# Opening of a decoder trunk: token tiles rounded one k tile at a time, two weight units loaded in pieces, outputs on two queues

## The chip, the cores and the metric

The kernel runs on one core of a Trainium2 chip. A core has a matrix engine (TensorE, PE in the profile), a vector engine (VectorE, DVE), an activation engine (ScalarE, ACT), a general engine (GpSimd, POOL) and a synchronisation engine (SyncE, SP) that here issues most memory transfers. Each engine takes its instructions in order; they wait for one another through semaphores. The metric is the time of one execution on the device in microseconds (us).

## The reference

A two-layer decoder over 256 tokens of width 1024. Every layer has two half-step SwiGLU networks around a token mixer, and each sub-layer is normalised on both sides:

```python
def rms_norm(x, g):
    xf = x.astype(jnp.float32)
    y = xf * lax.rsqrt(jnp.mean(xf * xf, axis=-1, keepdims=True) + EPS)
    return (y * g.astype(jnp.float32)).astype(x.dtype)

def swiglu(x, w_gate, w_up, w_down):
    return (jax.nn.silu(x @ w_gate) * (x @ w_up)) @ w_down

for layer in range(DEPTH):
    if layer == N_A_LAYERS:
        k, v, c = shared_kv(h, kv_norm_g, w_kv, w_fgate, b_fgate)
    f = swiglu(rms_norm(h, ffn1_pre_g[layer]), ffn1_w_gate[layer], ffn1_w_up[layer], ffn1_w_down[layer])
    h = h + 0.5 * rms_norm(f, ffn1_post_g[layer])
    hn = rms_norm(h, mix_pre_g[layer])
    m = recurrent_block(hn, ...) if layer < N_A_LAYERS else forgetting_attention(hn, ..., k, v, c)
    h = h + rms_norm(m, mix_post_g[layer])
    f = swiglu(rms_norm(h, ffn2_pre_g[layer]), ffn2_w_gate[layer], ffn2_w_up[layer], ffn2_w_down[layer])
    h = h + 0.5 * rms_norm(f, ffn2_post_g[layer])
```

The model width is 1024, the network width 2816. Everything is float32. The part that matters here is the very first product, the first network's `x @ w_gate` on normalised tokens, and the very last step, the sum into `h` that is the output.

## The kernel before

**Precision by two parts.** A float32 product is formed from three products of rounded operands. Each operand is split into an upper part (the value rounded to TensorE's format, `F32R`) and a lower part (the value minus its upper part, also rounded). The sum of upper by upper, upper by lower and lower by upper goes into one PSUM bank. ScalarE writes the upper part (a copy with rounding), VectorE the lower part (a subtraction).

**Tokens.** The 256 tokens are two halves (t = 0 and 1) of 128 rows, `h[0]` and `h[1]`. For a projection a half is turned on TensorE, 128 columns (one k tile) at a time, into a PSUM bank `gt` that holds four k tiles; there are two such banks. Then VectorE multiplies the four k tiles by the norm's weight `gT` into a scratch tile `xg` (L221), ScalarE rounds `xg` into `xhi` (L222), and VectorE writes `xlo` (L227). The root mean square itself is applied behind the product, as a factor per row (`stat`: a sum of squares on ScalarE, L204, then two small operations on GpSimd).

**Weights.** Weights come as units (items): a unit is two k tiles of 512 columns, 512 KB. It lands in one of five `raw` tiles, is split into `whi` and `wlo` (nine buffers each) by L174 and L175, and is used by both token halves, six products for each half. Each product is a 128x512 matrix product. Four units make one 128x512 result; the first four units are the first 512 columns of the first gate matrix, the next four those of the up matrix. Behind the opening the loop `run` walks the units with token half 0 ahead of half 1; in the first network half 0 takes units 4 to 7 before half 1 takes unit 4. A planner (`prepare_next`, with a modelled time `pace`, and `landed` and `split_at` for each unit) decides where in the program the split of a unit stands. TensorE's order is always the order of the program; in the opening that holds for all engines (`manual_schedule`).

**The opening** (L1091 to L1164) is an order written out by hand for the first four units and all sixteen token k tiles. SyncE loads the left half of `h[0]`, unit 0 in two pieces, the left half of `h[1]`, unit 1, the right half of `h[0]`, unit 2, the right half of `h[1]`, unit 3. The gain row (8 KB) is loaded by ScalarE's queue (L112). TensorE begins with four products on a zero tile (`keep_busy`, L126), turns the gain row, turns four k tiles of half 0, does three more zero products, and then goes through unit 0 and unit 1 by the strings in `FIRST`, each of which names a product by k tile in the unit, weight part and token part ("0ul" is k tile 0, upper weight, lower token). `turn_between` puts the transposes of the other four-tile groups between those products. Units 2 and 3 go through the ordinary `mm3`. The sums of squares stand behind the split of unit 3, and the split of unit 4 (L174) behind them. Then the two gate results go through SiLU (L474).

**The end.** `enter` with `last` forms the output rows in four pieces of 256 columns for each half (L259) and SyncE stores each piece (L261).

Of the kernel before, what the change touches and what calls it, by code (L numbers as in the profile page):

```python
# [9 lines left out]
F32 = mybir.dt.float32  # L10
# [6 lines left out]
P = 128  # L17
# [27 lines left out]
def trunk_kernel(ctx: ExitStack, tc: tile.TileContext, A: dict, out: bass.AP):  # L45
# [66 lines left out]
    nc.scalar.dma_start(grow0, A["ffn1_pre_g"].rearrange("l (k p) -> (l k) p", p=P))  # L112
# [6 lines left out]
    warm = cpool.tile([P, 1], F32, name="warm")  # L119
    nc.scalar.activation(warm, mhalf, AF.Silu)  # L120

    def keep_busy(n):
# [120 lines left out]
    def enter(t, dests, pf, gb, half, last=False, normed=False):  # L243
# [13 lines left out]
        for c in range(0, D, m):  # L257
            hn = h[t][:, c:c + m]
            nc.vector.scalar_tensor_tensor(hn, t1[c // 512][:, c % 512:c % 512 + m], r[:, 0:1], hn, ALU.mult, ALU.add)  # L259
            if last:  # L260
                nc.sync.dma_start(out[0, t * P:(t + 1) * P, c:c + m], hn)  # L261
        urgent.__exit__(None, None, None)
# [38 lines left out]
    def gain_bcast(src):  # L301
# [10 lines left out]
    OPEN = 4  # L312

    FIRST = {(0, 0): "0uu 0lu 0ul 1uu 1ul 1lu", (0, 1): "0uu 1uu 0ul 1ul 0lu 1lu",
             (1, 0): "0uu 1uu 0lu 1lu 0ul 1ul", (1, 1): "0uu 1uu 0lu 1lu 0ul 1ul"}
    between = {}
    first_loads = []
    landed = {}

# [41 lines left out]
    def proj_items(w, c0, nn, get_x, post, nk=8):  # L361
# [4 lines left out]
        for k0 in range(0, nk, kper):  # L366
# [7 lines left out]

            def work(t, u, k0=k0, kn=kn, i=len(items)):
                if k0 == 0:
                    acc[t] = mmbank()
                ps = acc[t][:, :nn]
                if (t, i) in FIRST:
                    for n, (j, a, b) in enumerate(FIRST[t, i].split()):  # L380
                        if (t, i, n) in between:
                            between.pop((t, i, n))()
                        j = int(j)
                        nc.tensor.matmul(ps, get_x(t, k0 + j)[b == "l"], (u.lo if a == "l" else u.hi)[:, j * nn:(j + 1) * nn],
                                         start=i == n == 0, stop=False)
                    return
# [5 lines left out]
            if not items:  # L392
                first_loads.append(lambda fetch=fetch: fetch(pieces=2))
            elif len(items) < OPEN:
                first_loads.append(fetch)
# [706 lines left out]
    def first_split(i, pieces=1):  # L1102

        u = units[i] = Unit()
        u.hi, u.lo = [wpool.tile([P, 1024], F32R, tag=s, name=nm(s), bufs=WB) for s in ("whi", "wlo")]
        m = 1024 // pieces

        def upper(c=0):
            nc.scalar.activation(u.hi[:, c * m:c * m + m], raws[i][:, c * m:c * m + m], AF.Copy)

        def lower(c=0):
            nc.vector.tensor_tensor(u.lo[:, c * m:c * m + m], raws[i][:, c * m:c * m + m],
                                    u.hi[:, c * m:c * m + m].bitcast(F32), ALU.subtract)
        return upper, lower

    dest = [main_dest(0, t) for t in range(2)]
    state["p"] = 2
    keep_busy(4)
    gains_T(grow0, 16, 0)
    tp00 = to_tp(h[0], 0)  # L1120
    keep_busy(3)
    upper, lower = first_split(0, 2)
    upper(0)
    x00 = x_upper(tp00, dest[0], 0)
    lower(0)
    x_lower(x00, dest[0], 0)
    upper(1)
    lower(1)
    tps = {}

    def turn_between(key, t, n):
        between[key] = lambda: tps.setdefault((t, n), to_tp(h[t], n))

    turn_between((0, 0, 3), 1, 0)
    half(0, 0)
    upper, lower = first_split(1)
    upper()
    lower()
    x10 = x_upper(tps[1, 0], dest[1], 0)
    turn_between((0, 1, 4), 0, 1)  # L1140
    half(0, 1)
    x_lower(x10, dest[1], 0)
    upper, lower = first_split(2)
    upper()
    x01 = x_upper(tps[0, 1], dest[0], 1)
    lower()
    turn_between((1, 0, 4), 1, 1)
    half(1, 0)
    x_lower(x01, dest[0], 1)
    x11 = x_upper(tps[1, 1], dest[1], 1)  # L1150
    half(1, 1)
    x_lower(x11, dest[1], 1)
    upper, lower = first_split(3)
    upper()
    lower()
    stat(0)
    stat(1)
    state["p"] = OPEN
    for i in range(OPEN):
        landed[i] = split_at[i] = pace["t"] - 2.0  # L1160
    for i in range(2, OPEN):
        half(0, i)
        half(1, i)
# [89 lines left out]
```

## Time and profile before

| | |
|---|---|
| runs | 1005.61, 1007.07 and 3560.49 us; median 1007.07 |
| profiled execution | 1005.73 us, of which the profile's span is 1004.0 |
| TensorE busy | 992.4 us of the span (99%) |
| VectorE, ScalarE busy | 618.1 us (62%), 529.9 us (53%) |
| data moved | 178.88 MB, mean 178 GB/s |
| first product of the opening | at 6.50 us |
| last product | begins at 997.04 us |

Times in the profile count from the start of the span. A timeline row gives the start, the duration, the engine, the line of the kernel, the operation with its output and inputs, the shape, and in brackets how long the engine had been idle and what released it. "PEld" is the weight load of TensorE; a matrix product's recorded duration overlaps with the next one, so the distance between two starts is what one product costs in a row. "SPq" and "ACTq" rows are transfers being issued, not moved. A group row gives the count, then the busy time and the mean duration in nanoseconds.

### The profile page before, as it was taken

The numbers are of one execution on the slowest core, as the hardware profiler recorded it, in microseconds if no ns is written. First come the engines' busy times: TensorE is split into PE (matmuls) and PEld (weight loads), VectorE is DVE, ScalarE is ACT, GpSimd is POOL, SyncE is SP. The second block draws the span as 40 slices with busy tenths as digits, with TensorE's granted clock in tenths as the row PEclk, the third lists the DMA queues.
The fourth block names the chain that finished last, engine by engine and source line by source line (L and its number), as shares of the span: only waits on it lengthen the run. The fifth ranks groups of instructions, "written<-read, shape, count | busy, mean of one in ns | idle before, by whom it ended". The sixth has DMA issues, their size and how long they took to land.

```text
span 1004.0 us, 12890 instructions
## 1 busy us (share of the span) xinstructions
PE 992.4 (99%) x4790; PEld 829.1 (83%) x4790; DVE 618.1 (62%) x761; ACT 529.9 (53%) x726; POOL 48.5 (5%) x94
## 2 busy tenths in 40 slices
PE   8999999999999999999999999999999999999997
PEld 5888888889988888888898888888888888888885
DVE  5756554668998555554686655554488475555542
ACT  6546443559986544443564444444466565444431
POOL 2400000000004000000100000000020000000000
PEclk9999999999999999999999999999999999999999
DMA  7877656565337766655567666555555067665531
GB/s 250 302 206 206 195 181 193 170 179 150 123 99 231 209 189 179 196 178 190 133 198 233 185 184 186 179 185 190 166 180 158 2 207 211 184 192 187 181 116 42
DMA packets 92628, 178.88 MB, mean 178 GB/s; under 512 B 11950, under 2 KB 32598, under 8 KB 92566
## 3 DMA queue, kind: packets, MB, share of 16 engines
q1 hardware_dynamic: 91702, 177.94, 57.4%
q8 instruction: 37, 0.61, 0.2%
q0 software_dynamic: 832, 0.12, 0.1%
q14 instruction: 25, 0.20, 0.1%
q10 hardware_dynamic: 32, 0.01, 0.0%
HBM read 176.95 MB, written 1.05 MB: 177 GB/s over the span
## 4 chain that ended last, share of the span: by engine, by line
PE 76%; issue 19%; ACT 2%; DVE 1%; POOL 1%; DMA 1%; SPq 0%; POOLq 0%; DVEq 0%; ACTq 0%
PE mm L182 22%; PE mm L184 22%; PE mm L183 22%; PE gt L717 2%; PE tr L489 1%; PE gt L1008 1%; PE mm L189 1%; PE mm L191 1%; PE mm L190 1%; PE mm L1035 1%; ACT junk L204 1%; DMA raw<-in_ffn_w_gate_dram 1%; PE gt L213 1%; PE tr L1024 0%; POOL rstd L199 0%
## 5 line engine op out<-in xcount | busy, mean ns | idle before, releaser
L175 DVE TENSOR_TENSOR wlo<-raw,whi 128x1024 fp32r<-128x1024 f32 (+4 forms) x329 | 395.7, 1207 | 269.5 <-ACT whi L174 267.8
L174 ACT ACTIVATE whi<-raw 128x1024 fp32r<-128x1024 f32 (+4 forms) x325 | 338.5, 1045 | 318.2 <-PE mm L184 254.0
L182 PE MATMUL mm<-whi,xhi 128*128 128x512 f32 (+2 forms) x776 | 307.6, 396 | 0.0
L184 PE MATMUL mm<-whi,xlo 128*128 128x512 f32 (+2 forms) x776 | 302.3, 390 | 0.0
L183 PE MATMUL mm<-wlo,xhi 128*128 128x512 f32 (+2 forms) x776 | 301.8, 389 | 0.2 <-DVE wlo L175 0.2
L184 PEld LDWEIGHTS mm<-whi,xlo 128*128 128x128 f32 x776 | 145.7, 188 | 30.7 <-DVE xlo L227 0.5
L183 PEld LDWEIGHTS mm<-wlo,xhi 128*128 128x128 f32 x776 | 146.1, 188 | 29.5 <-DVE wlo L175 1.2
L182 PEld LDWEIGHTS mm<-whi,xhi 128*128 128x128 f32 x776 | 145.9, 188 | 27.8
L182 PE MATMUL mm<-whi,hhi 128*128 128x512 f32 x352 | 139.2, 396 | 0.0
L184 PE MATMUL mm<-whi,hlo 128*128 128x512 f32 x352 | 137.9, 392 | 0.0
L183 PE MATMUL mm<-wlo,hhi 128*128 128x512 f32 x352 | 137.1, 389 | 0.0
L184 PEld LDWEIGHTS mm<-whi,hlo 128*128 128x128 f32 x352 | 66.1, 188 | 14.9
L183 PEld LDWEIGHTS mm<-wlo,hhi 128*128 128x128 f32 x352 | 66.2, 188 | 13.9
L182 PEld LDWEIGHTS mm<-whi,hhi 128*128 128x128 f32 x352 | 66.2, 188 | 13.1
L483 DVE SCALAR_TENSOR_TENSOR prod<-mm,rstd,sil 128x512 f32<-128x512 f32 (+1 forms) x48 | 33.9, 706 | 39.5 <-PE mm L184 35.8
L197 POOL TENSOR_SCALAR nv<-ss 128x1 f32<-128x1 f32 x24 | 11.6, 482 | 911.3 <-ACT junk L204 911.3
L474 ACT ACTIVATE sil<-mm,rstd 128x512 f32<-128x512 f32 (+1 forms) x48 | 31.3, 651 | 40.3 <-PE mm L184 40.3
L493 ACT ACTIVATE hhi<-tr 128x512 fp32r<-128x512 f32 (+1 forms) x48 | 26.6, 554 | 15.2 <-PE tr L489 15.1
L254 DVE TENSOR_TENSOR t<-mm,gb 128x512 f32<-128x512 f32 x24 | 16.2, 687 | 28.7 <-ACT junk L204 28.7
L204 ACT ACTIVATE junk<-mm 128x512 bf16<-128x512 f32 x24 | 14.2, 590 | 32.9 <-PE mm L184 32.8
L494 DVE TENSOR_TENSOR hlo<-tr,hhi 128x512 fp32r<-128x512 f32 (+1 forms) x48 | 30.5, 642 | 1.3
L182 PE MATMUL mm<-whi,zhi 128*128 128x340 f32 (+2 forms) x80 | 28.4, 355 | 0.0
(181 smaller groups left out, 907.1 us busy)
## 6 DMA issues: line engine op xcount, KB each, us to landing
raw<-in_ffn_w_down_dram SPq DMA_DIRECT2D x88, 512.0 KB
raw<-in_ffn_w_up_dram SPq DMA_DIRECT2D x80, 512.0 KB
raw<-in_ffn_w_gate_dram SPq DMA_DIRECT2D x79, 512.0 KB
raw<-in_rg_w_in_dram SPq DMA_DIRECT2D x20, 504.0 KB
raw<-in_rg_w_out_dram SPq DMA_DIRECT2D x10, 504.0 KB
raw<-in_ffn_w_gate_dram SPq DMA_DIRECT2D x18, 256.0 KB
raw<-in_ffn_w_up_dram SPq DMA_DIRECT2D x16, 256.0 KB
raw<-in_w_kv_dram SPq DMA_DIRECT2D x8, 512.0 KB
```

The source lines that it names most:

```text
L174: nc.scalar.activation(hi[:parts, c:c + m], rawv[:, c:c + m], AF.Copy)
L175: nc.vector.tensor_tensor(lo[:parts, c:c + m], rawv[:, c:c + m], hi[:parts, c:c + m].bitcast(F32), ALU.subtract)
L182: nc.tensor.matmul(ps, xh, wh, start=first, stop=False)
L183: nc.tensor.matmul(ps, xh, wl, start=False, stop=False)
L184: nc.tensor.matmul(ps, xl, wh, start=False, stop=last)
L204: nc.scalar.activation(junk[:, :src.shape[1]], src, AF.Square, scale=f, accum_out=acc)
L254: nc.vector.tensor_tensor(t1[n], pf[n], gb[:, n * 512:(n + 1) * 512], ALU.mult)
L474: nc.scalar.activation(s[:, :nn], ps, AF.Silu, scale=rs[t][:, 0:1])
L483: nc.vector.scalar_tensor_tensor(pr[:, :nn], ps, rs[t][:, 0:1], s, ALU.mult, ALU.mult)
L493: nc.scalar.activation(hv, tp[:, :nn], AF.Copy)
L494: nc.vector.tensor_tensor(lv, tp[:, :nn], hv.bitcast(F32), ALU.subtract)
L717: nc.tensor.matmul(ps[:w, j * S:(j + 1) * S], wv[:, o:o + w], xc[:w, k, :], start=k == 0, stop=k == m - 1)
```

## The change

The rest of the kernel keeps its order; on every engine only the opening and the last stores differ.

- `load_h` now takes k tile bounds and a queue. Half 0's left half is loaded in two pieces of two k tiles with the pieces of unit 0 between them; units 0 and 1 are loaded in pieces of one k tile. The left half of `h[1]` is loaded by ScalarE's queue, behind the warm-up activation.
- Tokens: the scratch tile `xg` is gone. ScalarE rounds each k tile on its own, straight from PSUM, with the norm's weight as the activation's scale (`x_up`); VectorE forms the lower part in one fused operation per k tile, again from PSUM (`x_lo`): sixteen operations on each engine.
- Weights of units 0 and 1 are split in pieces of one k tile; the upper part of the first piece of each is written by VectorE (`w_up(..., dve=True)`), not ScalarE.
- Products of all four units go by a written order (`products`). The first group of transposes is cut in two (`turn(0, 0, 2)` and `turn(0, 2, 4)`), the second standing behind the first two products. One zero product instead of three stands behind the first transposes, and only the half of the zero tile that is read is cleared.
- The splits of units 4 and 5 stand ahead of the sums of squares, that of unit 6 behind them, all three ahead of the two SiLUs.
- At the end, for half 1, the second and fourth of the four stores are issued by ScalarE's queue.

```diff
-    def load_h(t, n):
-        nc.sync.dma_start(h[t][:, n * 512:(n + 1) * 512], A["x"][0, t * P:(t + 1) * P, n * 512:(n + 1) * 512])
+    def load_h(t, a, b, q=nc.sync):
+        q.dma_start(h[t][:, a * P:b * P], A["x"][0, t * P:(t + 1) * P, a * P:b * P])
...
-    nc.vector.memset(idle, 0.0)
+    nc.vector.memset(idle[:, :512], 0.0)
...
     nc.scalar.activation(warm, mhalf, AF.Silu)
+    load_h(1, 0, 4, nc.scalar)
...
             if last:
-                nc.sync.dma_start(out[0, t * P:(t + 1) * P, c:c + m], hn)
+                q = nc.scalar if t == 1 and c % 512 else nc.sync
+                q.dma_start(out[0, t * P:(t + 1) * P, c:c + m], hn)
...
-    load_h(0, 0)
-    raws = [first_loads[0]()]
-    load_h(1, 0)
-    raws.append(first_loads[1]())
-    load_h(0, 1)
-    raws.append(first_loads[2]())
-    load_h(1, 1)
-    raws.append(first_loads[3]())
...
+    load_h(0, 0, 2)
+    load_w(0, 0, 1)
+    load_h(0, 2, 4)
+    load_w(0, 1, 2)
+    load_w(1, 0, 1)
+    load_w(1, 1, 2)
+    load_h(0, 4, 8)
+    load_w(2, 0, 2)
+    load_h(1, 4, 8)
+    load_w(3, 0, 2)
...
+    def w_up(i, a, b, dve=False):
+        c = slice(a * 512, b * 512)
+        if dve:
+            nc.vector.tensor_copy(parts[i][0][:, c], raws[i][:, c])
+        else:
+            nc.scalar.activation(parts[i][0][:, c], raws[i][:, c], AF.Copy)
...
+    def x_up(t, a, b):
+        for k in range(a, b):
+            nc.scalar.activation(xhi[:, k, t * P:(t + 1) * P], tps[t, k // 4][:, k % 4 * P:(k % 4 + 1) * P], AF.Copy,
+                                 scale=gT[:, k:k + 1])
+
+    def x_lo(t, a, b):
+        for k in range(a, b):
+            nc.vector.scalar_tensor_tensor(xlo[:, k, t * P:(t + 1) * P], tps[t, k // 4][:, k % 4 * P:(k % 4 + 1) * P],
+                                           gT[:, k:k + 1], xhi[:, k, t * P:(t + 1) * P].bitcast(F32),
+                                           ALU.mult, ALU.subtract)
+
+    def products(t, i, order):
+        for c in order.split():
+            j = int(c[0])
+            k = 2 * i + j
+            tensor_work(512)
+            nc.tensor.matmul(first_acc[t], main_x(t, k)[c[2] == "l"], parts[i][c[1] == "l"][:, j * 512:(j + 1) * 512],
+                             start=k == 0 and c[1:] == "uu", stop=k == 7 and c == order.split()[-1])
+
     keep_busy(4)
     gains_T(grow0, 16, 0)
-    tp00 = to_tp(h[0], 0)
-    keep_busy(3)
...
+    turn(0, 0, 2)
+    keep_busy(1)
+    x_up(0, 0, 2)
+    w_up(0, 0, 1, dve=True)
+    x_lo(0, 0, 1)
+    w_lo(0, 0, 1)
+    w_up(0, 1, 2)
+    x_lo(0, 1, 2)
+    w_lo(0, 1, 2)
+    products(0, 0, "0uu 0ul")
+    turn(0, 2, 4)
+    products(0, 0, "0lu 1uu 1ul 1lu")
+    turn(1, 0, 4)
+    x_up(1, 0, 2)
+    w_up(1, 0, 1, dve=True)
+    x_lo(1, 0, 2)
+    x_up(0, 2, 4)
+    w_lo(1, 0, 1)
+    products(1, 0, "0uu 0lu 1uu 1lu 0ul 1ul")
+    w_up(1, 1, 2)
+    x_lo(0, 2, 4)
+    x_up(1, 2, 4)
+    w_lo(1, 1, 2)
+    products(0, 1, "0uu 0lu 1uu 0ul 1ul")
+    turn(0, 4, 8)
+    products(0, 1, "1lu")
+    x_lo(1, 2, 4)
+    products(1, 1, "0uu 0lu 1uu 1lu 0ul 1ul")
+    w_up(2, 0, 2)
+    x_up(0, 4, 8)
+    w_lo(2, 0, 2)
+    turn(1, 4, 8)
+    x_lo(0, 4, 8)
+    products(0, 2, "0uu 1uu 0lu 1lu 0ul 1ul")
+    x_up(1, 4, 6)
+    w_up(3, 0, 2)
+    x_up(1, 6, 8)
+    x_lo(1, 4, 6)
+    w_lo(3, 0, 2)
+    x_lo(1, 6, 8)
+    products(1, 2, "0uu 1uu 0lu 1lu 0ul 1ul")
+    products(0, 3, "0uu 1uu 0ul 1ul 0lu 1lu")
+    products(1, 3, "0uu 1uu 0lu 1lu 0ul 1ul")
+    state["p"] = OPEN
+    for i in range(OPEN):
+        landed[i] = split_at[i] = pace["t"] - 3.0
+    for i in range(2):
+        prepare_next(True)
     stat(0)
     stat(1)
+    prepare_next(True)
...
```

`load_w(i, a, b)` loads k tiles a to b of unit i, `w_lo` writes the lower part of such a piece, `turn(t, a, b)` turns k tiles a to b of half t.

More of the change, by code (lines that the diff above doesn't have):

```diff
@@ L391, in work @@
                     post(t, acc[t][:, :nn])
-            if not items:
-                first_loads.append(lambda fetch=fetch: fetch(pieces=2))
-            elif len(items) < OPEN:
+            if len(items) < OPEN:
                 first_loads.append(fetch)
@@ new lines, in trunk_kernel, with w_lo @@
+    load_w(2, 0, 2)
+    load_h(1, 4, 8)
+    load_w(3, 0, 2)
+    parts = [[wpool.tile([P, 1024], F32R, tag=s, name=nm(s), bufs=WB) for s in ("whi", "wlo")] for _ in range(OPEN)]
+    def w_up(i, a, b, dve=False):
[4 more added lines that the diff above has]
+            nc.scalar.activation(parts[i][0][:, c], raws[i][:, c], AF.Copy)
+    def w_lo(i, a, b):
+        c = slice(a * 512, b * 512)
+        nc.vector.tensor_tensor(parts[i][1][:, c], raws[i][:, c], parts[i][0][:, c].bitcast(F32), ALU.subtract)
@@ new lines, in trunk_kernel, with turn @@
+    tps = {}
+    def turn(t, a, b):
+        n = a // 4
+        if (t, n) not in tps:
+            tps[t, n] = gtbank()
+        for k in range(a, b):
+            nc.tensor.transpose(tps[t, n][:, k % 4 * P:(k % 4 + 1) * P], h[t][:, k * P:(k + 1) * P], ident)
+    def x_up(t, a, b):
[3 more added lines that the diff above has]
+    def x_lo(t, a, b):
+        for k in range(a, b):
+            nc.vector.scalar_tensor_tensor(xlo[:, k, t * P:(t + 1) * P], tps[t, k // 4][:, k % 4 * P:(k % 4 + 1) * P],
+                                           gT[:, k:k + 1], xhi[:, k, t * P:(t + 1) * P].bitcast(F32),
+                                           ALU.mult, ALU.subtract)
@@ L1122, in trunk_kernel @@
[L1122 to L1142, printed above, removed]
@@ L1156, in trunk_kernel @@
     stat(0)
     stat(1)
-    state["p"] = OPEN
+    prepare_next(True)
     for i in range(OPEN):
-        landed[i] = split_at[i] = pace["t"] - 2.0
-    for i in range(2, OPEN):
+        units[i] = Unit()
         half(0, i)
```

46 lines of the change are left out of this document (10 added, 36 removed).

## The prediction

> **What bounds the kernel now.** I read the stretches first, then the timeline of the opening, then the groups that price single operations. The stretches (start and end, length, then busy time of each engine with its count, granted clock, DMA share, GB/s) show where TensorE idles:
>
> ```profile
> 0.00:20.00 20.00, 16.52 (x65) 10.37 (x66) 10.62 (x15) 10.41 (x16) 1.52 (x10) 1.00 0.75 263
> 20.00:28.00 8.00, 7.84 (x33) 5.73 (x32) 5.95 (x5) 6.85 (x8) 7.46 (x15) 1.00 0.76 211
> 28.00:100.00 72.00, 72.00 (x332) 59.27 (x331) 46.37 (x63) 39.48 (x45) 7.74 (x13) 1.00 0.77 239
> 100.00:990.00 890.00, 888.65 (x4333) 748.00 (x4332) 549.12 (x668) 471.05 (x653) 30.09 (x53) 1.00 0.56 173
> 990.00:1004.00 14.00, 7.44 (x33) 5.78 (x31) 6.07 (x12) 2.06 (x6) 1.72 (x4) 0.84 0.23 75
> ```
>
> From 28 to 990 us TensorE is busy 960.65 of 962. What can move lies in the first 28 us and in the last ten. So I follow one quantity: when TensorE reaches a fixed product behind the opening. I take the one at 27.86, the first after unit 7's first half; if it comes earlier, so does the end, since nothing behind it waits. The timeline (start, duration, engine, line, operation, in brackets the idle time before it and its releaser):
>
> ```profile
> 0.79 0.42 ACTq L112 DMA_DIRECT2D grow<-in_ffn_pre_g_dram  x1
> 2.53 0.20 ACT L120 ACTIVATE warm<-mhalf 128x1 f32<-128x1 f32 x1
> 3.65 0.26 PE L132 MATMUL tr<-ident,grow 16*128 16x16 f32 x1 [0.24 <-DMA grow<-in_ffn_pre_g_dram]
> 3.94 0.17 DVE L133 TENSOR_SCALAR gT<-tr 128x16 f32<-128x16 f32 x1 [2.48 <-PE tr L132]
> 3.94 1.12 PE L213 MATMUL gt<-ident,h 128*128 128x128 f32 x4
> 4.60 0.63 ACT L1109 ACTIVATE whi<-raw 128x512 fp32r<-128x512 f32 x1 [1.86 <-DMA raw<-in_ffn_w_gate_dram]
> 4.85 1.49 PE L126 MATMUL tr<-idle 128*128 128x512 bf16 x3
> 6.50 0.50 PE L384 MATMUL mm<-whi,xhi 128*128 128x512 f32 x1 [0.17 <-ACT xhi L222]
> 7.56 0.65 PE L213 MATMUL gt<-ident,h 128*128 128x128 f32 x4
> 8.28 0.39 PE L384 MATMUL mm<-whi,xlo 128*128 128x512 f32 x1
> 8.51 0.40 PE L384 MATMUL mm<-wlo,xhi 128*128 128x512 f32 x1
> 9.93 0.73 PE L384 MATMUL mm<-whi,xhi 128*128 128x512 f32 x2 [1.03 <-ACT whi L1109]
> 10.96 0.60 PE L213 MATMUL gt<-ident,h 128*128 128x128 f32 x4
> 11.32 0.71 PE L384 MATMUL mm<-wlo,xhi 128*128 128x512 f32 x2
> 12.46 0.73 PE L384 MATMUL mm<-whi,xhi 128*128 128x512 f32 x2 [0.42 <-ACT xhi L222]
> 16.64 1.04 ACT L1109 ACTIVATE whi<-raw 128x1024 fp32r<-128x1024 f32 x1
> 17.59 1.04 ACT L204 ACTIVATE junk<-h 128x1024 bf16<-128x1024 f32 x1
> 18.75 1.06 ACT L204 ACTIVATE junk<-h 128x1024 bf16<-128x1024 f32 x1
> 19.81 1.04 ACT L174 ACTIVATE whi<-raw 128x1024 fp32r<-128x1024 f32 x1
> 20.76 0.67 ACT L474 ACTIVATE sil<-mm,rstd 128x512 f32<-128x512 f32 x1
> 21.33 1.05 ACT L174 ACTIVATE whi<-raw 128x1024 fp32r<-128x1024 f32 x1
> 21.62 0.39 PE L182 MATMUL mm<-whi,xhi 128*128 128x512 f32 x1
> 22.17 0.50 PE L183 MATMUL mm<-wlo,xhi 128*128 128x512 f32 x1 [0.16 <-DVE wlo L175]
> 27.17 0.39 PE L182 MATMUL mm<-whi,xhi 128*128 128x512 f32 x1
> 27.86 0.39 PE L182 MATMUL mm<-whi,xhi 128*128 128x512 f32 x1
> ```
>
> Three products take 27.86 - 27.17 = 0.69, so 0.23 each. Between 6.50 and 27.86 stand 72 products (16.6 us) and three groups of four transposes, 0.36 each (10.96 to 11.32): 17.7 of 21.4 us. The other 3.7 are waits: for the second unit's weights (9.93), for the second token half's rounding (12.46), for the lower parts of units 4 to 6 (22.17 and two more). Ahead of 6.50 a chain runs: gain row, four transposes, scaling, rounding, first product.
>
> **The change part by part.** Prices of the new small pieces, from groups (count, then busy time, mean ns) and two timeline rows of the attention stage:
>
> ```profile
> L1016 ACT ACTIVATE pe<-gt,mx 128x128 f32<-128x128 f32 x16 | 5.6, 360 | 4.8 <-DVE mx L1011 4.8
> L483 DVE SCALAR_TENSOR_TENSOR prod<-mm,rstd,sil 128x256 f32<-128x256 f32 x8 | 3.9, 482 | 3.7 <-ACT sil L474 3.7
> L172 DVE CAST whi<-raw 128x1024 fp32r<-128x1024 f32 x4 | 2.7, 686 | 0.0
> L1112 DVE TENSOR_TENSOR wlo<-raw,whi 128x1024 fp32r<-128x1024 f32 x3 | 3.7, 1222 | 2.4 <-ACT whi L1109 2.4
> L1112 DVE TENSOR_TENSOR wlo<-raw,whi 128x512 fp32r<-128x512 f32 x2 | 1.4, 684 | 0.0
> ...
> 752.85 0.35 ACT L1016 ACTIVATE pe<-gt,mx 128x128 f32<-128x128 f32 x1
> 753.10 0.19 ACT L1016 ACTIVATION_READ_ACCUMULATOR pe<-gt,mx 128x1 f32 x1
> ```
>
> A scaled rounding of one k tile (L1129 in the new listing) is a 128x128 ScalarE read from PSUM: 0.36 long, and the next may start 0.25 later (752.85 to 753.10). I take 0.26 a piece in a row; ends 0.25 and 0.36. Its lower part is a 128x128 fused VectorE operation, unseen; 256 wide it takes 0.48, so 0.17 (a 16-wide one, L133) to 0.48 bounds it; I take 0.35, 0.27 in a row. The 512-wide VectorE copy lies between 0.34 (half of 0.686) and 0.69; I take 0.42. ScalarE thus gets sixteen pieces, 4.2 us, for four roundings of 0.63; VectorE loses four 512-wide scalings and gets sixteen small pieces for four lower parts.
>
> Step 1, first product. The gain row is still seen at 3.65. Two transposes instead of four end at about 3.94 + 0.56 = 4.50. ScalarE rounds k tile 0 from 4.55 to 4.91. The weight piece was usable at 4.60 behind 256 KB of tokens; now 128 KB are ahead of it, so not later: copy 4.60 to 5.02. First product at 5.05 instead of 6.50. The shorter memset and the dropped dummies lie in front of the gain row's landing and cost nothing unless the clock needs them (below).
>
> Step 2, unit 0. VectorE runs k tile 0's lower part (it waits for both ScalarE pieces of that bank, 5.18) to 5.56, the weight's lower half to 6.1, k tile 1's lower part to 6.45, the second lower half to 7.05. The transposes of k tiles 2 and 3 write the same bank and wait for 6.45; behind them in TensorE's order stand four products and the second token half's transposes. So: two transposes 6.5 to 6.8, products at 6.85, 7.1, 7.3, 7.55. The sixth came at 8.51.
>
> Step 3, rest of the opening. The second half's transposes start at 7.8 (7.56 before), end at 8.4, rounding to 8.75, its first product at 8.8. Then 42 products at 0.23 (9.66), two transpose groups (0.72) and about 0.2 of waiting for k tiles 4 and 5 of half 1, whose VectorE pieces wait for all four ScalarE pieces of the bank: unit 4 begins at 19.4 instead of 21.62.
>
> Step 4, what is late next. ScalarE's order is now: four pieces of half 1 around the rounding of unit 3, units 4 and 5, both square sums, unit 6, two SiLUs, unit 7. The last transposes come 18 products and one group after 8.8, at 13.3, and end at 13.9. From 13.95: 4 x 0.26, four roundings at 0.95 (16.64 to 17.59), square sums 2.22 (17.59 to 19.81), SiLUs 2 x 0.57 (20.76 to 21.33), unit 7 1.05: 23.2. VectorE's lower part 1.22: 24.47. TensorE reaches unit 7 at 19.4 + 18 x 0.23 = 23.5, issues one product and waits until 24.5; the fixed product follows 0.33 + 4 x 0.23 = 1.25 later, at 25.75. Against 27.86: **2.1 us earlier**. Two SiLUs ahead of unit 7 thus give back about 0.75.
>
> Loads: SyncE issues ten opening transfers instead of nine, in pieces, so unit 4's load goes out about 0.43 later; it is wanted only at about 16. Slot waits of the load queue are for transfers that end earlier: nothing. Half 1's left tokens move to ScalarE's queue, issued at 2.73 when that engine has nothing else: nothing, if they land by 7.8 (first rival).
>
> Step 5, outputs. The last rows:
>
> ```profile
> 999.30 1.67 DVE L259 SCALAR_TENSOR_TENSOR h<-t,rstd,h 128x256 f32<-128x256 f32 x4 [0.35 <-POOL rstd L199]
> 1000.71 0.89 SPq L261 DMA_DIRECT2D out_dram<-h  x2
> ...
> 6.00:7.00 1.00, 0.83 (x3) 0.30 (x2) 0.90 (x2) 0.97 (x2) 0.00 (x0) 1.00 0.95 328
> ```
>
> The last piece is ready at 1000.97; SyncE's last issue ends at 1001.60. From a free queue it would end at 1000.97 + 0.05 + 0.42 = 1001.44: 0.15 gained. At worst ScalarE's queue starts data later and loses 0.4; at best two queues' landings overlap and 0.4 is gained. I take 0.1.
>
> Sum: 2.1 + 0.1 = 2.2 from the profiled execution's 1005.73 (span 1004.0): **1003.5**. That execution stands 0.1 above the lowest of the three runs and 1.3 below their median; I forecast against it.
>
> [...]
>
> **The rivals.**
>
> Late tokens (slower than before). TensorE takes instructions in order, so half 1's transposes, if their tokens aren't there, hold everything behind them, one us per us beyond 7.8; from 9.9 on the kernel is slower than before, and at 11 it is at 1006.8. For it: the only transfer on ScalarE's queue, 8 KB, was issued at 0.79 and used at 3.65. Against: 2.73 + 2.86 = 5.6, plus 256 KB at 328 GB/s (6:7), 0.8, doubled where both queues share, is 7.2 at most. 12%.
>
> Small pieces make ScalarE the bound. At 0.36 each in a row the pieces ahead of 13.9 and the four behind it add about 0.7: 1004.2. [...] 10%.
>
> The clock rises later. Three dummies from 4.85 take 1.49, about 0.45 each; the products of 8.28 and 8.51 stand 0.23 apart: full speed came in between, ahead of most products. With fewer dummies it may come later. If only at 10, about eleven products cost 0.22 more each, 2.4, of which roughly 1.1 hides in waits: 1004.8. 10%. [...] The profile's clock column reads 1.00 throughout and can't decide it.
>
> The gain doesn't reach the end, or the first product isn't earlier: 1005.7. For it: units 8 and later need loads at a DMA share of 0.77. Against: no TensorE idle from 28 to 100. 6%.
>
> **How the numbers follow.** Forecast 62%, rivals 12, 10, 10 and 6. The range runs from 1001.4 to 1006.9. Its low end: without any wait TensorE would get from 5.05 to the fixed product with 17.7 us, at 22.8, 2.9 better than step 4; ScalarE's order forbids most of that, so I allow two thirds with the tail's best case left in. Its high end is late tokens at 11. Two per cent, 20 us, is about what a measurement of this kernel can tell from no change; no case comes near it: within 2% 0.95, slower 0.04 and faster 0.01 for what none of the cases names.
>
> **What would show it.** First product near 5.05; half 1's first product near 8.8 without a DMA in front; unit 4 near 19.4; a wait for unit 7's lower part near 24.5 where before units 4 to 6 waited; the fixed product near 25.75 and TensorE full behind it. Wrong if half 1's transposes wait for a DMA, if products before 10 us stand 0.43 apart, or if the stretches behind 28 us show new idle time.

## The result, and the profile after

The changed kernel takes **1007.23 us** (median of 22 runs, 1006.36 to 1008.84), the kernel before 1005.67 on the same chip (median of 22 runs). The ratio is 1.0014 (95% interval 1.0007 to 1.002): slower by 1.4 us by that ratio, far less than 2%, but clear of no change, while 1003.5 had been forecast and 1006.9 was the top of the range. The profiled execution took 1007.18 (span 1005.3); before it was 1005.73 (span 1004.0).

First the stretches of the kernel after (start and end, length, busy time of each engine with its count, granted clock, DMA share, GB/s):

```profile
0.00:20.00 20.00, 16.67 (x63) 11.12 (x64) 10.09 (x26) 11.11 (x25) 0.73 (x7) 1.00 0.78 263
20.00:28.00 8.00, 6.79 (x29) 5.12 (x29) 5.34 (x7) 6.90 (x10) 6.80 (x11) 1.00 0.78 252
28.00:100.00 72.00, 72.00 (x329) 59.22 (x329) 46.29 (x63) 39.25 (x45) 11.16 (x20) 1.00 0.76 234
100.00:990.00 890.00, 888.61 (x4335) 747.61 (x4334) 549.85 (x667) 471.01 (x652) 30.17 (x53) 1.00 0.56 173
```

From 28 to 990 TensorE is as full as before (960.61 us against 960.65). From 20 to 28 it is busy for 6.79 instead of 7.84: the loss of 1.05 stands there. Before 20 nothing was won to pay for it (16.67 against 16.52). The timeline of the kernel after (start, duration, engine, line, operation, in brackets idle time and releaser) shows how:

```profile
1.32 0.37 ACTq L110 DMA_DIRECT2D h<-in_x_dram  x1
4.15 0.63 PE L128 MATMUL tr<-idle 128*128 128x512 bf16 x1
5.24 0.43 DVE L1109 CAST whi<-raw 128x512 fp32r<-128x512 f32 x1 [1.28 <-DMA raw<-in_ffn_w_gate_dram]
5.81 0.77 PE L1144 MATMUL mm<-whi,xhi 128*128 128x512 f32 x1 [1.02 <-DVE whi L1109]
...
8.18 0.63 PE L1144 MATMUL mm<-whi,xlo 128*128 128x512 f32 x1
8.61 0.63 PE L1144 MATMUL mm<-wlo,xhi 128*128 128x512 f32 x1
9.03 1.05 PE L1125 MATMUL gt<-ident,h 128*128 128x128 f32 x4
10.12 1.15 ACT L1129 ACTIVATE xhi<-gt,gT 128x128 fp32r<-128x128 f32 x4 [3.03 <-PE gt L1125]
10.54 0.57 PE L1144 MATMUL mm<-whi,xhi 128*128 128x512 f32 x1 [0.46 <-ACT xhi L1129]
10.95 0.39 PE L1144 MATMUL mm<-wlo,xhi 128*128 128x512 f32 x1
11.18 0.40 PE L1144 MATMUL mm<-whi,xhi 128*128 128x512 f32 x1
...
19.70 0.60 DVE L1134 SCALAR_TENSOR_TENSOR xlo<-gt,gT,xhi 128x128 fp32r<-128x128 f32 x2
20.22 2.35 DVE L177 TENSOR_TENSOR wlo<-raw,whi 128x1024 fp32r<-128x1024 f32 x2
21.60 1.40 POOL L201 TENSOR_TENSOR rstd<-nv,mhalf 128x1 f32<-128x1 f32 x1
21.79 0.39 PE L184 MATMUL mm<-whi,xhi 128*128 128x512 f32 x1
23.10 1.23 DVE L177 TENSOR_TENSOR wlo<-raw,whi 128x1024 fp32r<-128x1024 f32 x1 [0.54 <-ACT whi L176]
23.29 1.46 POOL L201 TENSOR_TENSOR rstd<-nv,mhalf 128x1 f32<-128x1 f32 x1
24.79 0.69 ACT L468 ACTIVATE sil<-mm,rstd 128x512 f32<-128x512 f32 x1 [1.07 <-POOL rstd L201]
26.47 0.49 PE L184 MATMUL mm<-whi,xhi 128*128 128x512 f32 x1 [0.44 <-ACT whi L176]
27.73 0.50 PE L185 MATMUL mm<-wlo,xhi 128*128 128x512 f32 x1 [0.77 <-DVE wlo L177]
29.00 0.40 PE L184 MATMUL mm<-whi,xhi 128*128 128x512 f32 x1
...
998.20 0.40 PE L186 MATMUL mm<-whi,hlo 128*128 128x512 f32 x1
```

The reader is to see four things.

- Half 1's left tokens were issued on ScalarE's queue at 1.32, not at 2.73, and VectorE sees the first weight piece only at 5.24. The first product is at 5.81 (forecast 5.05).
- Up to 8.61 products stand 0.43 apart, from 10.95 on 0.23. In the kernel before the 0.23 came by 8.28. Half 1's first product, forecast for 8.8, is at 10.54.
- Unit 4 begins at 21.79, 0.17 later than before and 2.4 later than forecast.
- GpSimd's power operation (`rstd`), 0.57 long in the kernel before, lasts 1.40 and 1.46 while VectorE works on a lower part. SiLU 1 waits 1.07 for it, and unit 7, behind that SiLU on ScalarE, is late on TensorE twice (26.47 and 27.73). The fixed product is at 29.00 instead of 27.86 or the forecast 25.75.

### The profile page after: what moved, and what is told of

Same layout as the page of the kernel before. It is cut to its first block, busy times and chain, and to the rows that moved or that the text cites. A ratio compares the mean times of both kernels' runs of the same rounds, so it can differ in the third digit from the quotient of the medians.

```text
span 1005.3 us, 12910 instructions
## 1 busy us (share of the span) xinstructions
PE 992.7 (99%) x4788; PEld 829.8 (83%) x4788; DVE 617.7 (61%) x772; ACT 531.0 (53%) x737; POOL 50.6 (5%) x94
## 3 DMA queue, kind: packets, MB, share of 16 engines
HBM read 176.95 MB, written 1.05 MB: 177 GB/s over the span
## 4 chain that ended last, share of the span: by engine, by line
PE 76%; issue 19%; ACT 2%; POOL 1%; DVE 1%; DMA 0%; POOLq 0%; DVEq 0%; SPq 0%; ACTq 0%
PE mm L184 22%; PE mm L186 22%; PE mm L185 22%; PE gt L711 2%; PE tr L483 1%; PE gt L1002 1%; PE mm L191 1%; PE mm L193 1%; PE mm L192 1%; PE mm L1029 1%; PE mm L1144 1%; POOL rstd L201 1%; ACT junk L206 1%; PE gt L215 1%; ACT whi L176 1%
## 5 line engine op out<-in xcount | busy, mean ns | idle before, releaser
L184 PE MATMUL mm<-whi,xhi 128*128 128x512 f32 (+2 forms) x768 | 304.3, 396 | 0.4 <-ACT whi L176 0.4
L185 PE MATMUL mm<-wlo,xhi 128*128 128x512 f32 (+2 forms) x768 | 298.1, 388 | 0.8 <-DVE wlo L177 0.8
L186 PE MATMUL mm<-whi,xlo 128*128 128x512 f32 (+2 forms) x768 | 298.8, 389 | 0.0
```

What stands on the lines that cost most here:

```text
L184: nc.tensor.matmul(ps, xh, wh, start=first, stop=False)
L185: nc.tensor.matmul(ps, xh, wl, start=False, stop=False)
L186: nc.tensor.matmul(ps, xl, wh, start=False, stop=last)
```

## The experiments

Three theories were to be told apart, and the texts written before the runs call them by letters. **P**: GpSimd's powers stretch while VectorE works on a lower part, because the sums now stand behind units 4 and 5. **C**: TensorE reaches full speed, products 0.23 apart instead of 0.43, later. **D**: half 1's tokens on ScalarE's queue delay the first weight piece. Times are medians; the runs came in five groups, on several chips, and the kernel before ran beside each group, with medians of 1005.61, 1005.84, 1005.92, 1005.84 and 1005.52. Differences of a few tenths of a us between groups are not read. Each timeline is that of a single execution.

### One cause at a time, from the kernel after

**Sums first.** In the kernel after, both sums stand ahead of the splits of units 4 and 5 again.

```diff
-    for i in range(2):
-        prepare_next(True)
     stat(0)
     stat(1)
-    prepare_next(True)
+    for i in range(3):
+        prepare_next(True)
```

> The changed kernel with both sums of squares ahead of the splits of units 4 and 5. Theory P (GpSimd's small power operations run long while VectorE works on the lower parts of units 4 and 5, and the second SiLU and unit 7 wait for them): the power operations fall from 1.40 and 1.46 us to about 0.57, the long wait for unit 7 (26.47 and 27.73) goes, small waits at units 4 to 6 come back as in the kernel before, the first product behind unit 7 comes at 27.7 instead of 29.0, and the time falls by about 1.3 us, to about 1005.9. Theory C (the late clock alone costs the time): the opening up to 21.79 is the same, and the time stays at about 1007.2.

Measured: 1005.9 (1005.19 to 1007.33), 1.3 below the kernel after. Its timeline:

```profile
19.75 0.60 DVE L1134 SCALAR_TENSOR_TENSOR xlo<-gt,gT,xhi 128x128 fp32r<-128x128 f32 x2
20.00 0.57 POOL L201 TENSOR_TENSOR rstd<-nv,mhalf 128x1 f32<-128x1 f32 x1
20.86 0.57 POOL L201 TENSOR_TENSOR rstd<-nv,mhalf 128x1 f32<-128x1 f32 x1
21.82 0.39 PE L184 MATMUL mm<-whi,xhi 128*128 128x512 f32 x1
23.03 1.25 ACT L468 ACTIVATE sil<-mm,rstd 128x512 f32<-128x512 f32 x2
27.93 0.39 PE L184 MATMUL mm<-whi,xhi 128*128 128x512 f32 x1
```

Both powers take 0.57, the SiLUs stand back to back, the fixed product is 1.07 earlier with unit 4 at the same time (21.82 against 21.79). So the order of the sums costs the kernel after about 1.1 to 1.3 us, by way of the powers. What is left is the kernel before's time: without P the new opening wins nothing.

**Three zero products** in place of one behind the first transposes.

```diff
-    keep_busy(1)
+    keep_busy(3)
```

> The changed kernel with three zero products behind the first transposes, as before, instead of one. Theory C (TensorE's 1.0 us gap ahead of its first product keeps the clock low until about 10.5): products stand 0.23 apart from about 6.5 to 7.5 on instead of 0.43 until 9, unit 4 begins at about 20.5 instead of 21.8, and the time falls by 1.0 to 1.3 us, to about 1006. Theory P alone: no change, 1007.2, since unit 7 is held by GpSimd's results whatever TensorE does before. [...]

Measured: 1006.98, no change from the kernel after beyond its spread. Products stood 0.23 apart a little earlier (transposes of 0.60 at 9.52, where the kernel after has 1.05 at 9.03), but in this run the weight piece was seen at 5.76 and the first product at 6.33, so half 1's first product stood at 10.57 again, and the powers still lasted 1.39 and 1.46. These zero products alone win nothing beyond the spread.

**Half 1's left tokens by SyncE**, behind unit 0's second piece.

```diff
-    load_h(1, 0, 4, nc.scalar)
...
     load_w(0, 1, 2)
+    load_h(1, 0, 4)
     load_w(1, 0, 1)
```

> The changed kernel with the left half of half 1's tokens issued by SyncE behind unit 0's pieces, as before, instead of by ScalarE's queue. Theory D (that 256 KB transfer, issued at 1.32 on a queue of its own, takes bandwidth from the first weight pieces): VectorE sees unit 0's first piece at about 4.6 instead of 5.24, the first product comes at about 5.2 instead of 5.81, ScalarE sees the second piece at about 5.5 to 6.3 instead of 6.47; the time falls by only 0.2 to 0.4 us since later waits remain. If the pieces are late for their own sake (1 KB token rows, more transfers), 5.24 and 6.47 stay.

Measured: 1007.31 (1007.02 to 1009.74). From its timeline:

```profile
4.02 0.43 DVE L1109 CAST whi<-raw 128x512 fp32r<-128x512 f32 x1 [0.23 <-DMA raw<-in_ffn_w_gate_dram]
4.66 0.80 PE L1144 MATMUL mm<-whi,xhi 128*128 128x512 f32 x1
12.86 0.63 PE L1144 MATMUL mm<-whi,xhi 128*128 128x512 f32 x1
13.28 0.63 PE L1144 MATMUL mm<-wlo,xhi 128*128 128x512 f32 x1
```

D is shown: the piece is there 1.22 earlier and the first product at 4.66. The gain did not arrive in the time. In this profile products still stand 0.42 apart at 13.28, unit 4 begins at 23.04 and the fixed product is at 30.23: the first product came earlier, but TensorE stayed slow for longer. This execution, 1008.45, is 1.1 above its kernel's median, so it shows how far the rise can slip, not what it does as a rule.

**All outputs by SyncE.**

```diff
-                q = nc.scalar if t == 1 and c % 512 else nc.sync
+                q = nc.sync
```

> The changed kernel with all output stores issued by SyncE, as before. Before, 7.0 us lay between the start of the last recorded product and the end of the span; in the changed kernel 7.1. If the second queue costs at the end, this returns to 7.0 and the time falls by 0.1 us; if it gains and something else costs, it grows by 0.1 to 0.3 us.

Measured: 1007.64, 0.4 above the kernel after. From the last product to the end of the span it takes 7.35, with two queues 7.1 (998.20 to 1005.3). So the second queue costs nothing and gains 0.24 in the profiles; the last pair of runs below repeats this.

### The late clock by itself

**The kernel before with one zero product** instead of three.

> The kernel before, with one zero product ahead of the opening instead of three; nothing else differs. [...] Rival (the rise does not hang on the zero products): products 0.23 apart from 8.3 on, unit 4 at 21.6, no change of time.

```diff
-    keep_busy(3)
+    keep_busy(1)
```

Measured: 1005.9, no change. Its timeline:

```profile
9.27 0.63 PE L384 MATMUL mm<-whi,xlo 128*128 128x512 f32 x1
9.70 0.63 PE L384 MATMUL mm<-wlo,xhi 128*128 128x512 f32 x1
21.19 0.39 PE L182 MATMUL mm<-whi,xhi 128*128 128x512 f32 x1
```

Fewer zero products did bring slower products: those of 9.27 and 9.70 still stand 0.43 apart, where the kernel before had 0.23 at 8.28, so the rival fails in the spacing. In the rest it holds: the time is the same and unit 4 is not later (21.19 against 21.62; ScalarE saw unit 1's weights at 8.39 here and at 8.83 there, so the two profiles can't be compared to a tenth). In the kernel before the slow products lie in front of waits that end on something else (1.03 idle ahead of 9.93, 0.42 ahead of 12.46). In the new opening hardly any wait of this kind is left behind the first product (0.46 ahead of 10.54), so less of the slow products is covered. That is an argument from the rows; no run changes the moment of full speed alone.

**Both moves at once** (sums first, half 1's tokens by SyncE), and the same **filled**: five first zero products instead of four, and one between unit 0's second product and the next transposes.

```diff
-    keep_busy(4)
+    keep_busy(5)
     gains_T(grow0, 16, 0)
...
     products(0, 0, "0uu 0ul")
+    keep_busy(1)
     turn(0, 2, 4)
```

> The kernel after, with the square sums ahead of the splits of units 4 and 5, and the left tokens of half 1 on SyncE's queue behind the first weight piece. Theory P (GpSimd's powers stretched): both powers at 0.57, no wait of unit 7. Theory D (half 1's tokens ahead of the first weight piece): first product near 4.7. Theory C: if full speed comes by about 10.5, unit 4 begins near 20.9 and the time is about 1005.0; if it comes only at 13.6, as in the kernel with half 1's tokens alone on SyncE's queue, unit 4 is near 23 and the time about 1007.0.

> The same as the kernel with both moves, with five zero products ahead of the first product instead of four, and one more zero product between unit 0's second product and the next transposes, so that TensorE stands idle less from 3.5 to 7. Theory C: products 0.23 apart from about 7 on, half 1's first product near 9.3, unit 4 at 20.2 to 20.5, the first product behind unit 7's first half near 26.3, and the time 1004.0 to 1004.5, below both kernels. Rival (the rise does not follow the filling): as the kernel without it, 1005.0 to 1007.0.

Measured: 1005.35 (1004.9 to 1006.78) without the filling and 1004.8 (1004.6 to 1006.74) with it. Timeline of the first:

```profile
22.39 0.39 PE L183 MATMUL mm<-whi,xhi 128*128 128x512 f32 x1
```

and of the filled one:

```profile
5.84 0.39 PE L127 MATMUL tr<-idle 128*128 128x512 bf16 x1
20.52 0.39 PE L183 MATMUL mm<-whi,xhi 128*128 128x512 f32 x1
26.57 0.39 PE L183 MATMUL mm<-whi,xhi 128*128 128x512 f32 x1
```

A zero product is recorded as 0.63 long in the kernel after (4.15) and as 0.39 at 5.84 here; in the kernel after the first product recorded as 0.39 stands at 10.95, about 5 us later. The profiles differ by 1.87 at unit 4, the medians by only 0.55, with intervals that overlap: the profiled execution without the filling (1006.58) was one of its longer ones. The filled kernel's median is 1.0 below the kernel before's; the interval of that ratio, 0.9985 to 1.0003, just takes in no change.

### Why the powers stretched

**Twelve more powers** on GpSimd behind the second one, beside sums first; their results are unused.

```diff
+    for i in range(12):
+        probe = spool.tile([P, 1], F32, tag="probe", name=nm("probe"), bufs=1)
+        nc.gpsimd.tensor_tensor(probe, rs[1], mhalf, ALU.pow)
```

> The kernel with the square sums first, with twelve more 128x1 powers on GpSimd behind the second half's, their results unused: work is added, none left out. Theory P (such a power stretches while VectorE works on a lower part): the powers that fall into VectorE's idle time take about 0.57 each, and one that falls into a lower part of units 4 to 6 (about 21.3 to 24.7) lasts until VectorE is done, 1.2 or more. Rival (they stretched in the kernel after for another reason, such as their input's arrival): all twelve at 0.57. The time itself, about 1006.0 to 1006.5, decides nothing, since GpSimd's later loads go out later.

Measured: 1012.05. The fixed product is only 0.19 later than with the sums first (28.12); the other 5 to 6 us arise little by little behind it, while TensorE is busy. Why is not shown, and nothing is read from them. The group row (duration in ns, least, median and greatest) and the timeline:

```profile
L1202 POOL TENSOR_TENSOR probe<-rstd,mhalf x12: 549/1057/1384, 21.7 to 33.3; 128x1 f32<-128x1 f32 x12
21.45 1.22 DVE L177 TENSOR_TENSOR wlo<-raw,whi 128x1024 fp32r<-128x1024 f32 x1 [0.91 <-ACT whi L176]
21.70 1.38 POOL L1202 TENSOR_TENSOR probe<-rstd,mhalf 128x1 f32<-128x1 f32 x1
22.59 2.35 DVE L177 TENSOR_TENSOR wlo<-raw,whi 128x1024 fp32r<-128x1024 f32 x2
25.43 0.55 POOL L1202 TENSOR_TENSOR probe<-rstd,mhalf 128x1 f32<-128x1 f32 x1
25.44 1.25 DVE L177 TENSOR_TENSOR wlo<-raw,whi 128x1024 fp32r<-128x1024 f32 x1 [0.50 <-ACT whi L176]
```

The rival (all at 0.57) is out. The power that starts at 21.70 ends at 23.08, 0.41 behind the end of the lower part that was under way (21.45 + 1.22 = 22.67), though VectorE had by then begun the next one; in the kernel after the two end at 23.00 and 24.75, 0.43 and 0.42 behind such ends (22.57 and 24.33). So in these rows a power waits for the lower part that is under way, not for all of them. What it meets at its start decides here: the one that starts at 25.43, 0.01 ahead of a lower part, takes 0.55, and with the sums first the power of 20.00 takes 0.57 beside token pieces (19.75 to 20.35), which read one of their two tensors from PSUM. VectorE's side shows next to nothing of it: the lower part that starts 0.01 behind a power takes 1.25, against 1.22 for the one at 21.45.

**The kernel before with the sums behind** the splits of units 4 and 5, this part of the change alone.

> The kernel before with one part of the change alone: both square sums behind the splits of units 4 and 5. Theory P (a power waits for VectorE's lower part that is under way): GpSimd's two powers last over 1.0 us instead of 0.57, unit 7's lower part comes late, the first product behind unit 7's first half lies at 28.5 to 29.2 instead of 27.86, and the time is 0.6 to 1.3 above the kernel before. Rival (the order costs only beside the pieces of the new opening): no change.

```diff
-    stat(0)
-    stat(1)
     state["p"] = OPEN
...
+    for i in range(2):
+        prepare_next(True)
+    stat(0)
+    stat(1)
```

Measured: **1004.74** (1004.28 to 1005.5), ratio 0.9989 (0.998 to 0.9998): the expectation had the wrong sign. Its timeline:

```profile
18.34 2.35 DVE L175 TENSOR_TENSOR wlo<-raw,whi 128x1024 fp32r<-128x1024 f32 x2
20.19 0.59 POOL L197 TENSOR_SCALAR nv<-ss 128x1 f32<-128x1 f32 x1 [18.83 <-ACT junk L204]
20.86 0.57 POOL L199 TENSOR_TENSOR rstd<-nv,mhalf 128x1 f32<-128x1 f32 x1
21.73 0.57 POOL L199 TENSOR_TENSOR rstd<-nv,mhalf 128x1 f32<-128x1 f32 x1
26.54 0.39 PE L182 MATMUL mm<-whi,xhi 128*128 128x512 f32 x1
```

Here VectorE is through with both lower parts at 20.69. GpSimd's operation ahead of the first power (L197, 0.23 long in the kernel before) starts at 20.19 and takes 0.59: the little that was left of the lower part stretches this one, and the power behind it finds VectorE idle. Units 4 to 6 no longer wait, and the fixed product is at 26.54, 1.32 earlier than before. Not all of this is the order: 0.52 of it stands at unit 4 already (21.10 against 21.62), where this execution saw unit 1's weights earlier (8.31 against 8.83); the waits behind unit 4 that have gone make 0.80. So the order of the change is a good one by itself. It turns against the kernel in the new opening, where VectorE begins these two lower parts only at 20.22: it still has unit 3's lower part and two pairs of token pieces to do (the last at 19.70). L197 starts at 21.03 there, with 1.5 us of lower parts still to come instead of 0.5, and the power meets the second of them.

**The filled opening with the sums behind**, that is, the kernel after with half 1's tokens by SyncE and the two zero products.

> The kernel after with half 1's left tokens on SyncE's queue and the two zero products more, but with the square sums left behind the splits of units 4 and 5. It takes the opening of the filled kernel and the order of the kernel after. If the three causes add: unit 4 begins near 20.5, GpSimd's powers still last 1.4 us, SiLU 1 and unit 7 still come late, the first product behind unit 7's first half is at about 20.5 + 7.2 = 27.7, and the time 1005.9, some 1.1 above the filled kernel with the sums first (1004.8). Rival (the sums' order only matters beside the slow opening): fixed product near 26.6 and 1004.8.

Measured: 1006.65. The powers last 1.39 and 1.46 again and SiLU 1 waits 1.07, as expected. The median is 1.85 above the filled kernel's, more than the 1.1 expected, and the fixed product is at 28.43, not 27.7. Two things make up the difference between the profiles: unit 4 begins at 21.24, 0.72 behind the filled kernel's 20.52, since the products stood 0.23 apart only from about 9 on, though TensorE's order up to there is the same; and from unit 4 to the fixed product it takes 7.19 instead of 6.05. So P's own part is 1.14, as with the sums first. Why the medians differ by more is not shown.

### A version that beats both

**Unit 4 ahead of the sums**: the filled kernel with half 1's k tiles 4 to 7 rounded in one go, and unit 4 alone ahead of the sums.

```diff
-    x_up(1, 4, 6)
+    x_up(1, 4, 8)
     w_up(3, 0, 2)
-    x_up(1, 6, 8)
...
+    for i in range(1):
+        prepare_next(True)
     stat(0)
     stat(1)
-    for i in range(3):
+    for i in range(2):
         prepare_next(True)
```

> The filled kernel (sums first, half 1's left tokens by SyncE, two more zero products) with two shifts on ScalarE: half 1's k tiles 4 to 7 rounded in one go ahead of unit 3's weights, and unit 4's upper part ahead of the square sums. Both waits that the filled kernel shows on TensorE between 16 and 22 (0.43 for a lower part of the tokens at 17.16, 0.45 for unit 4's at 21.20) should go: unit 4 near 20.1, no wait behind it, the first product behind unit 7's first half at 25.7 to 26.3 instead of 26.57, time 1004.0 to 1004.5. If a power then falls into unit 4's lower part (about 18 to 19.2), SiLU 1 comes late and the gain is lost: 1004.8 or more.

Measured: 1004.7. Unit 4 began at 20.08 as expected, but unit 5 then waited 0.6 for its own lower part, and the fixed product stayed at 26.58: the wait had moved by one unit.

**Two ahead, two behind**: as that, but units 4 and 5 ahead of the sums, 6 and 7 behind them, and the SiLUs behind unit 7.

```diff
-    for i in range(1):
+    for i in range(2):
         prepare_next(True)
     stat(0)
     stat(1)
     for i in range(2):
         prepare_next(True)
```

> The filled kernel with another order on ScalarE: half 1's k tiles 4 to 7 rounded in one go, units 4 and 5 ahead of the square sums (as in the kernel after), units 6 and 7 behind them and both ahead of the SiLUs. VectorE then has no backlog when the second power comes, and no SiLU stands ahead of unit 7. Worked out from the rows of the kernel with unit 4 ahead: unit 4 near 20.1, units 4 and 5 without a wait, unit 6's lower part 0.15 late, unit 7's near 24.4, the first product behind unit 7's first half at 25.7 to 25.9 instead of 26.57, the value that the prediction had given (25.75), and the time 1003.8 to 1004.1. The first power may stretch to 1.4 here, since a lower part lies beside it, and costs nothing, since the SiLUs stand behind two more splits. Rival (the first 27 us are bound elsewhere, or the shifted loads give it back): 26.5 and 1004.7, as in the three fastest kernels so far.

Measured: 1004.6 (1003.54 to 1007.04). The lowest run is where the expectation was, the profiled one isn't: in its timeline unit 0's products are still recorded as 0.63 long at 7.96.

```profile
7.96 0.63 PE L1144 MATMUL mm<-whi,xlo 128*128 128x512 f32 x1
26.49 0.39 PE L183 MATMUL mm<-whi,xhi 128*128 128x512 f32 x1
```

The fixed product stands where it stood in the two kernels ahead, for another reason: nothing waits in front of it any more except 0.18 at unit 6, but TensorE was slow for longer (a product is still recorded as 0.63 at 8.38, where that kernel has a zero product of 0.39 at 5.83), and unit 4 began at 20.73 instead of 20.08.

**The same, filled more densely**: one more zero product ahead of the first product, one behind half 1's first transposes.

```diff
     turn(0, 0, 2)
-    keep_busy(1)
+    keep_busy(2)
...
     turn(1, 0, 4)
+    keep_busy(1)
     x_up(1, 0, 2)
```

> The kernel with units 4 and 5 ahead of the square sums and 6 and 7 behind them, with two more zero products where TensorE still stands idle in the opening: one ahead of the first product, one behind half 1's first transposes. If filling decides when full speed comes: products 0.23 apart by 6 in the profile, half 1's first product by 9.4, unit 4 near 20.1, the first product behind unit 7's first half at 25.7 to 25.9, a median of 1003.6 to 1004.0 and a narrower spread than 1003.54 to 1007.04. Rival (the rise falls where it falls, whatever fills the gaps): runs spread as before, median 1004.6.

Its timeline:

```profile
7.86 0.39 PE L1144 MATMUL mm<-whi,xlo 128*128 128x512 f32 x1
26.15 0.39 PE L183 MATMUL mm<-whi,xhi 128*128 128x512 f32 x1
```

Measured: **1003.76** (1003.39 to 1005.09), ratio to the kernel before 0.9984 (0.9975 to 0.9993): 1.8 us below the kernel before of its group and 3.5 below the kernel after. Ten of eleven runs lie under 1004.5, where the less densely filled kernel had four; the intervals of the two ratios overlap. The filling seems to help, but doesn't settle the moment: the profiled run (1004.17) has full speed from about 7 on, not by 6.

**The dense kernel with all outputs by SyncE.**

> The same dense kernel with all outputs on SyncE's queue, as in the kernel before. By the prediction's step 5 it is 0.1 slower than the dense kernel with two queues, by the profiles of the kernel after and of its version with one queue (7.1 and 7.35 from the last product to the end) 0.25; rival: no difference.

Measured: 1004.03 (1003.79 to 1004.55), 0.27 above the dense kernel, with intervals that overlap almost wholly. In the profiles it takes 7.35 from the last product to the end with one queue and 7.1 with two, as in the kernel after and its version with one queue. Its profile has the fixed product at 25.51.

## Why the prediction was wrong, by its own steps

**What bounds the kernel** held: nothing behind 28 us moved, and the fixed product told the end. It came 1.14 later than before, and the profiled execution 1.45 later; of the rest 0.15 is the tail, and about 0.15 lies outside the profile's span.

**Step 1 failed in the weight piece.** "Now 128 KB are ahead of it, so not later" left out the 256 KB of half 1's tokens, whose issue it placed at 2.73, behind the warm-up activation. They were issued at 1.32, while ScalarE's table was still loading, and the piece was usable at 5.24 instead of 4.60. Without them it was 4.02 and the first product 4.66, earlier than forecast. So the term "nothing" for half 1's left tokens should have been about 0.6 to 1.2 us at the first weight piece; the first rival looked at the wrong victim, since the tokens were in time (the transposes at 9.03 name no DMA).

**Steps 2 and 3** priced every product at 0.23. They stood 0.43 apart until 8.61, and the last of unit 0 came 1.06 late, half 1's transposes 1.23, its first product 1.74. From there to unit 4 another 0.65 was lost (2.39 late), beyond the 0.2 of waiting that had been taken; one wait for a lower part of half 1's tokens, ahead of the product at 18.44, makes 0.4 of it. The rival "the clock rises later" named this and even its time (10), and had 10%. It deserved more: by step 2's own times TensorE has only two products to do between 5.05 and 6.5, and the change takes two zero products away, a step that by itself left the kernel before with products 0.43 apart at 9.27; as it ran, 1.02 of idle TensorE stood ahead of the first product besides. How many us of the time the late rise cost is worked out from rows, not shown by a run of its own. Nor is it shown what sets the moment: with the same TensorE order up to there the zero product behind unit 0's second product is recorded as 0.39 long in the filled kernel (5.84) and as 0.65 in the one with the sums behind (6.09), which records a product still as 0.63 at 8.24.

**The prices of the pieces were right.** Four ScalarE pieces in a row take 1.15 (4 x 0.26 had been taken), the 512-wide copy 0.43 (0.42), two token pieces on VectorE 0.60 (0.35 and 0.27 make 0.62). "Small pieces make ScalarE the bound" is out: it took 0.36 for each piece in a row, 1.44 for four.

**Step 4 left out GpSimd.** Its order of ScalarE was right, its sum of durations too. It did not follow GpSimd's two small operations, which stand between the square sums and the SiLUs: they were 0.57 and 0.56 before, where VectorE stood idle beside them (18.93 to 20.89), and the change moved VectorE's work under them. The 2.39 of unit 4 and another 0.86 behind it make the 3.25 by which the fixed product missed 25.75. With P cured alone it stood at 27.93, with the opening cured too at 26.57, with unit 7 ahead of the SiLUs at 25.51 in the best profile. So a time near the forecast was there to be had (median 1003.76, lowest run 1003.39 in the dense kernel), but not with this order.

**Step 5**: within one kernel two queues gain 0.24 in both pairs of profiles, and 0.4 and 0.27 in the medians: more than the 0.1 that was taken. Against the kernel before the way from the last product to the end is not shorter all the same: 7.1 after, 7.0 before, 7.35 with one queue in the new kernel. The traces show where that 0.4 goes. At the very end SyncE waits for its transfers one semaphore after the other, 0.06 apart. The view of its waits (total, times, longest) in the kernel before and in the kernel after with one queue:

```profile
SPq L1248 <- DMA out_dram<-h: 0.9, 2, 0.4
SPq L1289 <- DMA out_dram<-h: 1.4, 1, 1.4
```

The wait for the last output ends 6.0 behind the last product in both. In the kernel before it is the last but one of these waits; in the new kernel it is the second, and seven more follow it (6.02 to 6.45). The forecast had no term for this; why the last output's place in that order changed is not shown.

**The range** reached its high end by late tokens alone. The late clock and the stretched powers together went past it, and no case had added two of them.

## What to carry to other kernels

Follow every engine between a moved producer and its reader, however small its operation is: a 0.57 us power decided 1.1 to 1.3 us here, and whether it did hung on about 1 us of VectorE's timing. When a change removes waits from TensorE's first microseconds, ask what those waits had covered: slow products (0.43 apart up to 8.61 in the kernel after) were free before and, by the rows, on the path afterwards. A transfer on another queue is not free because its issuing engine is; ask which earlier-wanted transfer it delays, 1.22 us here.

## What the runs showed of the hardware

- A 128x1 GpSimd power of 0.55 to 0.57 lasted 1.04 to 1.46 when it started beside one of VectorE's 128x1024 subtractions of two SBUF tensors, and ended 0.41 to 0.43 behind the end of that one. Started 0.01 ahead of a subtraction, or beside 128x128 operations with one PSUM input, it stayed at 0.55 and 0.57. The subtractions kept their 1.21 to 1.25 throughout.
- A transfer that stands in the listing on ScalarE's queue behind an activation was issued at 1.32, while that engine's table load ran (1.25 to 2.53) and ahead of the activation (2.54). Whether the queue passed them or the compiled order had it first is not shown.
- The profile's clock column reads 1.00 from the start to 990 in the kernel after, but its products from 7.75 to 8.61 stand 0.43 apart, those from 10.95 on 0.23. In the new openings the change to 0.23 came by 5.5 to about 9 in the six profiles with filled gaps and later than 9, up to 13.7, in those without. Equal orders differ: the filled kernel has a zero product recorded as 0.39 long at 5.84, the one with the sums behind still a product of 0.63 at 8.24.
